# Strassen products on pairs of output stripes, with weight sums formed by adding DMAs, in a two-layer streaming-encoder kernel

## The chip, the cores and the metric

The kernel runs on one core of a Trainium2 chip, as one program. The metric is the device time of one execution in microseconds (us): 1938.96 as the median of three runs before the change (1936.39 to 1940.4). The engines that matter here are TensorE (PE; its weight loads are listed as PEld), VectorE (DVE), ScalarE (ACT), GpSimd (POOL) and SyncE (SP), which issues most DMAs. Every engine works through its own instructions in a fixed order and waits on semaphores for the others.

## The reference

A sequence of 512 positions with 16 meta tokens in front (528 rows of 2048 features) passes two layers, each with a norm ahead and a residual add behind, and a last norm.

```python
for layer in range(DEPTH):
    hn = rms_norm(h, norm_gain[layer])
    if layer % 2 == 0: y = even_mixer(...)   # ... concatenate([a_out, b_out]) @ w_out
    else:              y = odd_mixer(...)
    h = h + y
h = rms_norm(h, final_norm_gain)
return h[:, N_META:]
```

Layer 0 (even) joins a convolution branch with sparse attention and ends in a 2048 x 2048 output projection. Layer 1 (odd) is a gated linear recurrence of 16 heads with 128 features each. Its end is what the change is about:

```python
q, fz, i, g = split_last(hn @ w_in, (D_REC, D_REC, D_REC, D_REC))
...
o = o * lax.rsqrt(jnp.mean(jnp.square(o), -1, keepdims=True) + RMS_EPS)
o = o * norm_g.reshape(H_C, DV_C).astype(jnp.float32)
o = o.reshape(bsz, t_len, D_REC).astype(hn.dtype) * jax.nn.silu(g)
return o @ w_out
```

All of it is in float32, and 2048 x 2048 matrices are multiplied with that accuracy.

## The kernel before, in words

Activations lie transposed, features on the 128 partitions and positions along the row, as 16 tiles. A product with a 2048 x 2048 matrix is made of 16 *stripes*: one stripe is 128 output features, its weights are a 128 x 2048 float32 tile of 1 MB (16 blocks of 128 x 128), and its result is one PSUM bank of 512 columns or two of 264.

For accuracy each float32 operand is a pair of float16 numbers, hi and lo, and each block takes three matmuls: hi by hi, hi by lo, lo by hi (`stripe`, L233 to L235). So a stripe of layer 0 has 96 matmuls of 264 columns and a stripe of 512 positions 48 matmuls of 512 columns. What a stripe needs of its weights is done by `load`: SP fetches the tile into one of three buffers `w32` (L185); ACT squares it and sums each row (L193); POOL adds the rows' sums over the partitions (`all_sum`, L142); DVE makes a power-of-two scale and its inverse from that (L146, L199, L201); then in two halves of 1024 columns ACT writes hi, the scaled weights rounded to float16 (L207), and DVE writes lo, what is left over (L208). Tiles `wh` and `wl` have two buffers of 2048 columns. `split` (L275 on ACT, L276 on DVE) makes such pairs of activations.

The order of the work, by the profile's times: layer 0's mixer to about 740 us; its output projection, the loop at L709 over 16 stripes, to about 933. There DVE adds a finished stripe's two PSUM halves to the residual tile `h1` (L716), and ACT squares the result for layer 1's norm, into `acc1` for stripe 0 (L720) and into `sq1` for the others (L723). Its activations are the pairs `x`, split from 8 tiles `mb` and 8 tiles `z` ahead of it (L275, L276). Then the norm, the 16 recurrent heads to about 1590, 16 gate stripes to 1750.8 and layer 1's output projection. Every gate stripe is squared and scaled like any other, its sum going to a column of `gstat`; the gated heads `ON` are then split into the pairs `MO` (the name `on`) with a scale that needs all 16 sums. The output projection does stripes 0 to 13 one after another, 48 matmuls of 512 columns each; the residual comes back from `h1d` in memory by SP into a tile `fz`, DVE adds it (L977), and ACT squares the sum and applies the last gain (L983, L986). The last two stripes go in two halves of 256 columns (L1012 to L1014), with the final norm and the writing out of the first half beside the second.

Within a stage the order is set by a scheduler that works with bands of priority (`band(WGT)` for weights, `EVAC` for emptying PSUM, `SIDE`, `CONV`) and by pools with a fixed number of buffers: an instruction that writes a tile stands behind the readers of what the buffer held. The order is fixed when the program is built.

Of the kernel before, what the change touches and what calls it, by code (L numbers as in the profile page):

```python
# [11 lines left out]
F32 = mybir.dt.float32  # L12
# [62 lines left out]
def trunk_kernel(ctx: ExitStack, tc: tile.TileContext, x: bass.AP, w: bass.AP, wukv: bass.AP,  # L75
# [53 lines left out]
    warm_in = wpool.tile([128, 2048], F16, name="wl", bufs=2)[:, :512]  # L129
# [58 lines left out]
    def load(s, back, keep=None):  # L188

        w32 = load_raw(s)  # L190
        junk = wpool.tile([128, 2048], BF16, name="junk", bufs=1)
        ss = wpool.tile([128, 1], F32, name="ss", bufs=4)
        S.activation(junk, w32, AF.Square, accum_out=ss)  # L193
        total = wpool.tile([128, 1], F32, name="tot", bufs=4) if keep is None else keep
        all_sum(total, ss)
# [6 lines left out]
        sc, inv = sc.bitcast(F32), inv.bitcast(F32)  # L202
        hi = wpool.tile([128, 2048], F16, name="wh", bufs=2)
        lo = wpool.tile([128, 2048], F16, name="wl", bufs=2)
        for n in range(2):
            sl = slice(1024 * n, 1024 * (n + 1))
            S.activation(hi[:, sl], w32[:, sl], AF.Identity, scale=sc)  # L207
            V.scalar_tensor_tensor(lo[:, sl], w32[:, sl], sc, hi[:, sl], op0=OP.mult, op1=OP.subtract)  # L208
        return hi, lo, inv
# [7 lines left out]
    def stripe(s, X, back, wide=True, order=(0, 1), ring=None, keep=None):  # L217

        cols = columns(wide)
        ring = [r or bank for r in ring or (None, None)]  # L220
        parts = [(r(), sl) for r, sl in zip(ring, cols)]
        parts = [(p[:, :sl.stop - sl.start], sl) for p, sl in parts]
        with band(WGT):
            hi, lo, inv = load(s, back, keep)
        for n, half in enumerate(order):
            for o, sl in parts:
                for k in range(8):
                    kt = half * 8 + k
                    xh, xl = X[kt]
                    ws = slice(kt * 128, kt * 128 + 128)  # L230
                    if xh.shape[-1] == SEQ:
                        sl = slice(0, SEQ)
                    P.matmul(o, hi[:, ws], xh[:, sl], start=n == 0 and k == 0, stop=False)  # L233
                    P.matmul(o, hi[:, ws], xl[:, sl], start=False, stop=False)  # L234
                    P.matmul(o, lo[:, ws], xh[:, sl], start=False, stop=n == 1 and k == 7)  # L235
        return parts, inv
# [470 lines left out]
    back1 = xscale[1][1]  # L707
    H1 = []
    for n in range(KT):  # L709
# [4 lines left out]
        with band(EVAC):  # L714
            for p, sl in ps:
                V.scalar_tensor_tensor(hin[:, sl], p, inv, hin[:, sl], op0=OP.mult, op1=OP.add)  # L716
            H1.append(hin)
            Q.dma_start(h1d[n], hin)
            if n == 0:
                S.activation(acc1, hin, AF.Square)  # L720
# [71 lines left out]
    def rec_head(h, fz, q, v):  # L792
# [120 lines left out]
        on = ht([128, SEQ], F32, "on", 18)  # L913
# [43 lines left out]
    with band(SIDE):
        gs = ht([128, 2], F32, "gs")
        V.tensor_reduce(gs[:, 0:1], gstat, axis=AX, op=OP.add)
        V.scalar_tensor_tensor(gs[:, 0:1], gs[:, 0:1], 2049.0 * 128.1, vmax[:, 1:2], op0=OP.mult, op1=OP.mult)  # L960
# [3 lines left out]
        for h in range(16):  # L964
            MO.append(split(ht([128, 2, SEQ], F16, "on", 18), ON[h], gs[:, 1:2]))

    HS = SEQ // 2  # L970
# [3 lines left out]
    def add_square(n, ps, inv, sl, hin):  # L974

        h2 = H2[n]
        V.scalar_tensor_tensor(h2[:, sl], ps, inv, hin[:, sl], op0=OP.mult, op1=OP.add)  # L977
# [17 lines left out]
    for n in range(KT - 2):  # L995
        with band(EVAC):
            hin = residual(n)
        ps, inv = stripe(S_OO + n, MO, oback, wide=False)
        with band(EVAC):
            add_square(n, ps[0][0], inv, slice(0, SEQ), hin)  # L1000
    with band(WGT):
        hins = [residual(n) for n in (KT - 2, KT - 1)]
        W = {n: load(S_OO + n, oback) for n in (KT - 2, KT - 1)}
    for c in range(2):
        tk = slice(c * HS, (c + 1) * HS)
        for n in (KT - 2, KT - 1):
            p = main_ps.tile([128, 512], F32, name="mps", bufs=3)[:, :HS]
            hi, lo, inv = W[n]
            for k in range(KT):
                xh, xl = MO[k]  # L1010
                ws = slice(k * 128, k * 128 + 128)
                P.matmul(p, hi[:, ws], xh[:, tk], start=k == 0, stop=False)  # L1012
                P.matmul(p, hi[:, ws], xl[:, tk], start=False, stop=False)
                P.matmul(p, lo[:, ws], xh[:, tk], start=False, stop=k == KT - 1)  # L1014
            with band(EVAC):
                got = add_square(n, p, inv, tk, hins[n - KT + 2])
# [12 lines left out]
        with band(EVAC if c else SIDE):  # L1029
            at = 0  # L1030
            for g, size in enumerate((4, 4, 4, 2, 2) if c else (2,) * 8):
                if c == 0:
                    o = ht([128, T], F32, "fv"[g % 2], 2)
                elif g < 3:
                    o = wpool.tile([128, 2048], F32, name="w32", bufs=3)
                else:
                    o = wpool.tile([128, 2048], F16, name=("wh", "wl")[g - 3], bufs=2).bitcast(F32)
# [93 lines left out]
```

## Time and profile before

| | |
|---|---|
| median of three runs | 1938.96 us |
| the profiled execution | 1940.51 us, span 1938.7 us, granted clock 0.985 |
| PE busy | 1855.5 us, 96% |
| DVE busy | 1268.5 us, 65% |
| ACT busy | 1143.1 us, 59% |
| POOL busy | 145.2 us, 7% |
| HBM read | 177.38 MB |

Times within the profile are counted from the span's first instruction. A row of a group gives the line, the engine, the operation, what it writes and reads with buffer numbers left out, and behind the bar the busy time, the mean of one in ns, and the time that the engine had been idle just before, with what ended it. "L233 <-ACT" thus means that TensorE's matmul at line 233 had waited for ACT. A row of the time line gives the start, the duration and the instruction. Matmuls overlap, so the distance between two starts tells their price, and the duration in a row does not. Idle time of an engine other than the one that bounds a stage costs nothing.

### The profile page before, as it was taken

How to read it: one execution, taken by the hardware profiler on the slowest of the kernel's cores; microseconds unless marked ns; L12 is line 12 of the kernel's file. 1: busy time of each engine (PE TensorE's matmuls, PEld its weight loads, DVE VectorE, ACT ScalarE, POOL GpSimd, SP SyncE). 2: the span in 40 equal slices, each digit the busy share in tenths (PEclk: the TensorE clock that was granted, in tenths of full speed). 3: DMA queues.
4: the chain of work that ended last, by engine and by line, in shares of the span. 5: the costliest groups of instructions: out<-in, count | busy, mean ns of one | idle time of the engine just before them, and what ended most of it. 6: DMA issues, size and time to landing. Idle time of an engine off the chain costs nothing.

```text
span 1938.7 us, 35168 instructions
## 1 busy us (share of the span) xinstructions
PE 1855.5 (96%) x14430; PEld 1358.2 (70%) x14430; DVE 1268.5 (65%) x2729; ACT 1143.1 (59%) x1833; POOL 145.2 (7%) x294
## 2 busy tenths in 40 slices
PE   8999999799999898999899999999999999999997
PEld 6767568678888787888577777777777764444445
DVE  7588988896747355434677777677777774454335
ACT  6544565346565765434577776677767765465443
POOL 1100001011211210000100000000000000000000
PEclk9999999899999999999999999999999999999999
DMA  6322223234443235433222121221221222223333
GB/s 236 108 79 92 87 93 120 73 95 124 118 128 105 77 101 198 150 132 110 77 88 88 66 88 66 88 88 66 88 88 67 93 99 88 95 101 103 130 109 98
DMA packets 46722, 198.75 MB, mean 103 GB/s; under 512 B 5792, under 2 KB 13256, under 8 KB 27872
## 3 DMA queue, kind: packets, MB, share of 16 engines
q1 hardware_dynamic: 38000, 182.20, 26.9%
q0 software_dynamic: 8560, 14.30, 3.5%
q8 instruction: 113, 1.85, 0.4%
q14 instruction: 49, 0.40, 0.1%
HBM read 177.38 MB, written 11.22 MB: 97 GB/s over the span
## 4 chain that ended last, share of the span: by engine, by line
issue 52%; PE 18%; DMA 11%; DVE 9%; ACT 7%; POOL 3%; SPq 0%; POOLq 0%; ACTq 0%; DVEq 0%
DMA w<-in_w_dram 9%; DVE wl L208 5%; PE mps L233 4%; PE mps L234 4%; PE mps L235 4%; ACT junk L193 3%; POOL tot L142 2%; ACT wh L207 2%; DVE z L546 1%; PE po L600 1%; PE s L249 1%; DVE mask L512 1%; PE s L575 1%; DMA L<-bdram 0%; DVE mask L521 0%
## 5 line engine op out<-in xcount | busy, mean ns | idle before, releaser
L233 PE MATMUL mps<-x,wh 128*128 128x264 f16 (+1 forms) x3440 | 1021.0, 297 | 22.6 <-ACT gt L533 10.4
L234 PE MATMUL mps<-x,wh 128*128 128x264 f16 (+1 forms) x3440 | 1021.9, 297 | 5.7 <-DVE x L276 5.0
L235 PE MATMUL mps<-x,wl 128*128 128x264 f16 (+1 forms) x3440 | 1021.5, 297 | 0.0
L193 ACT ACTIVATE junk<-w 128x2048 bf16<-128x2048 f32 x144 | 275.1, 1910 | 493.5 <-DMA w<-in_w_dram 486.8
L234 PEld LDWEIGHTS <-wh 128*128 128x128 f16 x3680 | 362.2, 98 | 164.8 <-issue 26.4
L235 PEld LDWEIGHTS <-wl 128*128 128x128 f16 x3680 | 362.3, 98 | 159.8 <-issue 13.7
L233 PEld LDWEIGHTS <-wh 128*128 128x128 f16 x3680 | 362.3, 98 | 149.9 <-issue 9.6
L208 DVE SCALAR_TENSOR_TENSOR wl<-w,sc,wh 128x1024 f16<-128x1024 f32 x288 | 361.6, 1282 | 33.5 <-ACT wh L207 33.0
L207 ACT ACTIVATE wh<-w,sc 128x1024 f16<-128x1024 f32 x288 | 313.4, 1135 | 40.3 <-PE mps L234 39.7
L146 DVE TENSOR_SCALAR u<-tot 128x1 int32<-128x1 int32 x112 | 17.1, 152 | 286.1 <-POOL tot L142 286.0
L546 DVE SCALAR_TENSOR_TENSOR z<-u,vec,z 128x528 f32<-128x528 f32 x240 | 180.8, 763 | 2.7
L142 POOL PARTITION_ALL_REDUCE tot<-ss x112 | 44.7, 400 | 1185.6 <-ACT junk L193 1184.5
L235 PE MATMUL mps<-on,wl 128*128 128x512 f16 x224 | 85.0, 379 | 4.7 <-DVE wl L208 4.7
L233 PE MATMUL mps<-on,wh 128*128 128x512 f16 x224 | 84.9, 379 | 1.8 <-ACT on L275 1.4
L234 PE MATMUL mps<-on,wh 128*128 128x512 f16 x224 | 84.9, 379 | 0.0
L784 ACT ACTIVATE qhm<-q 128x256 f16<-128x256 f32 x128 | 51.8, 416 | 41.3 <-DVE q L886 41.3
L785 DVE SCALAR_TENSOR_TENSOR qlm<-q,qhm 128x256 f16<-128x256 f32 x128 | 52.3, 418 | 8.9 <-ACT qhm L784 8.6
L785 DVE SCALAR_TENSOR_TENSOR kt0l<-k,kt0h 128x512 f16<-128x512 f32 (+1 forms) x64 | 35.3, 551 | 24.5 <-ACT kt0h L784 24.4
L146 DVE TENSOR_SCALAR u<-gstat 128x1 int32<-128x1 int32 x16 | 2.4, 153 | 70.2 <-POOL gstat L142 70.2
L871 DVE COPY_PREDICATED A<-msk,s 128x256 f32<-128x256 uint8 x96 | 46.0, 479 | 0.8 <-PE s L790 0.8
L716 DVE SCALAR_TENSOR_TENSOR h<-mps,inv,h 128x264 f32<-128x264 f32 x32 | 15.5, 488 | 45.2 <-PE mps L235 45.2
L512 DVE SCALAR_TENSOR_TENSOR mask<-sq,wiT,mask 128x144 f32<-128x144 f32 (+3 forms) x80 | 36.6, 491 | 6.0 <-ACT sq L511 5.8
(365 smaller groups left out, 2394.2 us busy)
## 6 DMA issues: line engine op xcount, KB each, us to landing
w<-in_w_dram SPq DMA_DIRECT2D x146, 1024.0 KB, 4.9
h<-in_x_dram SPq DMA_DIRECT2D x16, 264.0 KB, 4.4
h1d<-h SPq DMA_DIRECT2D x16, 264.0 KB, 2.1
fz<-h1d SPq DMA_DIRECT2D x15, 256.0 KB, 2.6
z<-in_x_dram SPq DMA_DIRECT2D x8, 264.0 KB, 6.7
L<-bdram POOLq DMA_DIRECT2D x8, 264.0 KB, 3.8
L<-mask POOLq DMA_DIRECT2D x8, 264.0 KB, 3.4
mbd<-mb SPq DMA_DIRECT2D x8, 264.0 KB, 2.6
```

Source lines behind the costliest of these rows:

```text
L142: G.partition_all_reduce(out, src, channels=128, reduce_op=op or bass_isa.ReduceOp.add)
L193: S.activation(junk, w32, AF.Square, accum_out=ss)
L207: S.activation(hi[:, sl], w32[:, sl], AF.Identity, scale=sc)
L208: V.scalar_tensor_tensor(lo[:, sl], w32[:, sl], sc, hi[:, sl], op0=OP.mult, op1=OP.subtract)
L233: P.matmul(o, hi[:, ws], xh[:, sl], start=n == 0 and k == 0, stop=False)
L234: P.matmul(o, hi[:, ws], xl[:, sl], start=False, stop=False)
L235: P.matmul(o, lo[:, ws], xh[:, sl], start=False, stop=n == 1 and k == 7)
L512: V.scalar_tensor_tensor(M[t][:, s0:s1], r[:, :s1 - s0], wiT[:, t, h:h + 1], M[t][:, s0:s1], op0=OP.mult, op1=OP.add)
L546: eng.scalar_tensor_tensor(z, u[:, j:j + T], col(V_CW + i * CW + j), z, op0=OP.mult, op1=OP.add)
L784: S.activation(hi, src, AF.Copy, scale=scale)
L785: V.scalar_tensor_tensor(lo, src, scale, hi, op0=OP.mult, op1=OP.subtract)
L871: V.copy_predicated(A.rearrange("p b (n a m) -> p b n a m", a=2, m=mm)[:, :, :, 1, :], msk[:, li - 1 + i:li + i, :].rearrange("p b (n m) - ...
```

## The change

**Half buffers.** `load` is taken apart into `square_sum`, `scales` and `split_weights`; tiles `wh` and `wl` now hold 1024 columns and have five buffers each. This concerns all stripes of the kernel.

**Gate squares.** In layer 0's output projection each of the 16 stripes is followed by `gate_stat`: ACT's queue issues the load of one gate stripe's weights (1 MB, tile `gw`, two buffers), and ACT squares and sums them into a column of `gss`. One sum over the partitions for all 16 comes before the gate stage, whose stripes then take their scales from it (`known`) and are not squared again. They now go in the order 0, 8, 1, 9 and so on, and after each two of them `group` makes four pairs of operands: the two heads themselves (`MO`), and sums and differences of their halves of 256 positions (`FA`, `FB`).

**Strassen's scheme.** Stripes 0 to 13 of layer 1's output projection go in seven pairs. Two stripes, the two halves of the 2048 input features and the two halves of the 512 positions make a 2 x 2 by 2 x 2 block product, done with 7 products instead of 8; each is 8 blocks times three matmuls of 256 columns. The weight operands are the quarters w11 and w12 of the first stripe and w22 of the second, and the sums s1 = w21 + w22, s2 = s1 + w11, s4 = s2 + w12 and s3 = w11 + w21; the signs of the scheme lie with the activations' sums and with the adds behind the products. The sums are formed by DMAs that add what they bring to what lies in the tile, which GpSimd issues: s1, s2 and s4 one after the other in one tile `wt` (two buffers, for pairs n and n+1), so that L1072 must come behind the split of s1, and L1075 behind the split of s2. The residuals, all 16, are now brought by POOL's queue straight into the tiles `x` that hold the sums later (L1046), and each finished product is added to the places where it belongs, by DVE. The last two stripes and the tail are as before.

```diff
-        hi = wpool.tile([128, 2048], F16, name="wh", bufs=2)
-        lo = wpool.tile([128, 2048], F16, name="wl", bufs=2)
+        hi = wpool.tile([128, 1024], F16, name="wh", bufs=5)
+        lo = wpool.tile([128, 1024], F16, name="wl", bufs=5)
...
+    def gate_stat(h):
+        with band(CONV):
+            raw = U.tile([128, 2048], F32, name="gw", bufs=2)
+            S.dma_start(raw, w[S_G + h])
+            square_sum(raw, gss[:, h:h + 1])
...
+        gate_stat(n)
...
     def residual(n):
-        hin = ht([128, T], F32, ("fz", "fz", "k")[max(0, n - KT + 3)], 2)
-        Q.dma_start(hin[:, :SEQ], h1d[n, :, NM:])
         H2[n] = r2p.tile([128, SEQ], F32, name="x", bufs=KT)
-        return hin
+        G.dma_start(H2[n], h1d[n, :, NM:])
+
+    def pair_weights(sa, sb):
+
+        with band(WGT):
+            A_ = load_raw(sa)
+            tt = ht([128, 1024], F32, "wt", 2)
+            Q.dma_start(tt, w[sb, :, :1024])
+            G.dma_start(tt, w[sb, :, 1024:], accum_op=OP.add)
+            B_ = wpool.tile([128, 2048], F32, name="w32", bufs=3)
+            Q.dma_start(B_[:, 1024:], w[sb, :, 1024:])
+            Q.dma_start(B_[:, :1024], w[sa, :, :1024])
+            G.dma_start(B_[:, :1024], w[sb, :, :1024], accum_op=OP.add)
...
+            out["w11"] = split_weights(A_[:, :1024], sc)
+            out["s1"] = split_weights(tt, sc)
+            G.dma_start(tt, w[sa, :, :1024], accum_op=OP.add)
+            out["w12"] = split_weights(A_[:, 1024:], sc)
+            out["s2"] = split_weights(tt, sc)
+            G.dma_start(tt, w[sa, :, 1024:], accum_op=OP.add)
+            out["s3"] = split_weights(B_[:, :1024], sc)
+            out["w22"] = split_weights(B_[:, 1024:], sc)
+            out["s4"] = split_weights(tt, sc)
+        return out, inv, ninv
...
+        product(a, W["w11"], x11)
+        product(c, W["s1"], y1)
+        product(b, W["s2"], u2)
+        product(a, W["w12"], x21, start=False)
+        product(b, W["s3"], z3, start=False)
+        product(c, W["s4"], x22, start=False)
+        product(b, W["w22"], z4, start=False)
```

In the diff `w[sa]` and `w[sb]` are the two stripes of a pair; L1054, L1058, L1072 and L1075 are its four adding DMAs in the order in which they stand above, and L1053, L1056 and L1057 the plain loads by SP.

How this moves the instructions: at the start of layer 0's output projection ACT's order was this before. `h1_8496` is stripe 0's result, `w32_8748` and `w32_8873` belong to stripes 2 and 3; stripe 1's weights (`w32_8623`) were split further ahead, among the splits of `x`.

```order
L275 ACTIVATE x_8474<-z_4788,mxb_8400 128x528
L275 ACTIVATE x_8477<-z_5416,mxb_8400 128x528
L275 ACTIVATE x_8480<-z_6490,mxb_8400 128x528
L207 ACTIVATE wh_8761<-w32_8748,sc_8757 128x1024 x2
L720 ACTIVATE acc1_8495<-h1_8496 128x528
L207 ACTIVATE wh_8886<-w32_8873,sc_8882 128x1024 x2
L723 ACTIVATE sq1_8741<-h1_8619 128x528
L193 ACTIVATE junk_9125,ss_9126<-w32_9123 128x2048
```

And TensorE mixed stripe 1 (`mps_8621`) with stripe 0 (`mps_8498`, `mps_8499`), 28 matmuls of the one among the 96 of the other:

```order
L233 LDWEIGHTS wh_8513
L233 MATMUL mps_8499<-x_8459,wh_8513 128x264
L234 LDWEIGHTS wh_8636
L234 MATMUL mps_8621<-x_8456,wh_8636 128x264
L235 LDWEIGHTS wl_8637
L235 MATMUL mps_8621<-x_8456,wl_8637 128x264
```

After the change the same place of ACT's order reads as follows; `h1_8596` is stripe 0's result, `w32_8729` stripe 1's weights.

```order
L287 ACTIVATE x_8575<-z_5478,mxb_8498 128x528
L287 ACTIVATE x_8578<-z_6564,mxb_8498 128x528
L725 DMA gw_8721<-in_w_dram 128x2048
L725 DMA gw_8852<-in_w_dram 128x2048
L740 ACTIVATE acc1_8593<-h1_8596 128x528
L190 ACTIVATE junk_8723,gss_8594<-gw_8721 128x2048
L190 ACTIVATE junk_8732,ss_8731<-w32_8729 128x2048
L725 DMA gw_8983<-in_w_dram 128x2048
L190 ACTIVATE junk_8854,gss_8594<-gw_8852 128x2048
L206 ACTIVATE wh_8742<-w32_8729,sc_8738 128x1024
L206 ACTIVATE wh_8746<-w32_8729,sc_8738 128x1024
```

What moved: stripe 1's square and split now stand behind `acc1` of stripe 0 and two gate squares, and TensorE takes all of stripe 0 before the first matmul of stripe 1.

POOL's order in layer 1's output projection held one row per stripe before, the sum over the partitions:

```order
L142 ISA tot_21143<-ss_21141 128x1
L142 ISA tot_21219<-ss_21217 128x1
L142 ISA tot_21295<-ss_21293 128x1
L142 ISA tot_21371<-ss_21369 128x1
L142 ISA tot_21447<-ss_21445 128x1
```

After the change it holds the adding DMAs of two pairs at a time. `wt_21506` is the summing tile of pair 2, `wt_21757` of pair 3, `wt_22008` of pair 4; `w32_21760` and `w32_22011` hold s3 of pairs 3 and 4.

```order
L1054 DMA wt_21757<-in_w_dram 128x1024
L1072 DMA wt_21506<-in_w_dram 128x1024
L1058 DMA w32_21760<-in_w_dram 128x1024
L1075 DMA wt_21506<-in_w_dram 128x1024
L142 ISA tot_21773<-ss_21771 128x1
L1054 DMA wt_22008<-in_w_dram 128x1024
L1072 DMA wt_21757<-in_w_dram 128x1024
L1075 DMA wt_21757<-in_w_dram 128x1024
L1058 DMA w32_22011<-in_w_dram 128x1024
```

What moved: the first sum of the next pair stands ahead of the second sum of the running pair in every turn; in the first turn shown the next pair's s3 stands ahead of the running pair's s4 too (so for pairs 1, 2 and 4), in the second behind it (pairs 3 and 5). TensorE takes the products of a pair in the order w11, s1, s2, w12, s3, s4 (the last two partly mixed or exchanged), w22, the last mixed with w11 of the next pair.

More of the change, by code (lines that the diff above doesn't have):

```diff
@@ L186, in load_raw, with square_sum, scales @@
         return w32
-    def load(s, back, keep=None):
-        w32 = load_raw(s)
+    def square_sum(src, ss):
         junk = wpool.tile([128, 2048], BF16, name="junk", bufs=1)
[L192 to L195, printed above, removed]
+        S.activation(junk[:, :src.shape[-1]], src, AF.Square, accum_out=ss)
+    def scales(total, back):
         u = wpool.tile([128, 1], I32, name="u", bufs=4)
@@ L201, in load, with split_weights @@
         V.tensor_scalar(inv, u, back, None, op0=OP.add)
-        sc, inv = sc.bitcast(F32), inv.bitcast(F32)
-        hi = wpool.tile([128, 2048], F16, name="wh", bufs=2)
-        lo = wpool.tile([128, 2048], F16, name="wl", bufs=2)
[L205 to L209, printed above, removed]
+        return sc.bitcast(F32), inv.bitcast(F32)
+    def split_weights(src, sc):
+        hi = wpool.tile([128, 1024], F16, name="wh", bufs=5)
+        lo = wpool.tile([128, 1024], F16, name="wl", bufs=5)
+        S.activation(hi, src, AF.Identity, scale=sc)
+        V.scalar_tensor_tensor(lo, src, sc, hi, op0=OP.mult, op1=OP.subtract)
+        return hi, lo
+    def load(s, back, keep=None, known=None):
+        w32 = load_raw(s)
+        if known is None:
+            ss = wpool.tile([128, 1], F32, name="ss", bufs=4)
+            square_sum(w32, ss)
+            total = wpool.tile([128, 1], F32, name="tot", bufs=4) if keep is None else keep
+            all_sum(total, ss)
+            known = scales(total, back)
+        sc, inv = known
+        halves = [split_weights(w32[:, 1024 * n:1024 * (n + 1)], sc) for n in range(2)]
+        return [h[0] for h in halves], [h[1] for h in halves], inv
     def bank():
@@ L215, in columns, with stripe @@
         return (slice(0, HT), slice(HT, T)) if wide else (slice(NM, T),)
-    def stripe(s, X, back, wide=True, order=(0, 1), ring=None, keep=None):
+    def stripe(s, X, back, wide=True, order=(0, 1), ring=None, keep=None, known=None):
         cols = columns(wide)
@@ L223, in stripe @@
         with band(WGT):
-            hi, lo, inv = load(s, back, keep)
+            hi, lo, inv = load(s, back, keep, known)
         for n, half in enumerate(order):
@@ new lines, in pair_weights @@
+    def pair_weights(sa, sb):
[8 more added lines that the diff above has]
+            G.dma_start(B_[:, :1024], w[sb, :, :1024], accum_op=OP.add)
+            ss = wpool.tile([128, 3], F32, name="ss3", bufs=2)
+            for i, v in enumerate((A_, tt, B_[:, 1024:])):
+                square_sum(v, ss[:, i:i + 1])
+            s1 = wpool.tile([128, 1], F32, name="ss", bufs=4)
+            V.tensor_reduce(s1, ss, axis=AX, op=OP.add)
+            total = wpool.tile([128, 1], F32, name="tot", bufs=4)
+            all_sum(total, s1)
+            sc, inv = scales(total, oback)
+            ninv = wpool.tile([128, 1], F32, name="ninv", bufs=4)
+            V.tensor_scalar(ninv, inv, -1.0, None, op0=OP.mult)
+            out = {}
+            out["w11"] = split_weights(A_[:, :1024], sc)
[8 more added lines that the diff above has]
+        return out, inv, ninv
@@ new lines, in product, with cut @@
+    def product(p, ws, xs, start=True, stop=True, resume=True):
+        hi, lo = ws
+        for k in range(8):
+            sl = slice(k * 128, k * 128 + 128)
+            xh, xl = xs[k]
+            for i, (wt, xt) in enumerate(((hi, xh), (hi, xl), (lo, xh))):
+                P.matmul(p, wt[:, sl], xt, start=start and k == i == 0, stop=stop and k == 7 and i == 2,
+                         skip_group_check=stop and not start and resume)
+    def cut(X, sl):
+        return [(xh[:, sl], xl[:, sl]) for xh, xl in X]
@@ L1001, in trunk_kernel @@
+    for n in range(0, KT - 2, 2):
+        pair_stripes(n)
     with band(WGT):
-        hins = [residual(n) for n in (KT - 2, KT - 1)]
+        for n in (KT - 2, KT - 1):
+            residual(n)
         W = {n: load(S_OO + n, oback) for n in (KT - 2, KT - 1)}
@@ L1006, in trunk_kernel @@
         for n in (KT - 2, KT - 1):
-            p = main_ps.tile([128, 512], F32, name="mps", bufs=3)[:, :HS]
+            p = bank()[:, :HS]
             hi, lo, inv = W[n]
[L1009 to L1014, printed above, removed]
+            for half in range(2):
+                product(p, (hi[half], lo[half]), cut(MO[8 * half:8 * half + 8], tk), half == 0, half == 1, False)
             with band(EVAC):
-                got = add_square(n, p, inv, tk, hins[n - KT + 2])
+                V.scalar_tensor_tensor(H2[n][:, tk], p, inv, H2[n][:, tk], op0=OP.mult, op1=OP.add)
+                got = add_square(n, tk)
         with band(EVAC):
@@ L1032, in trunk_kernel @@
                 if c == 0:
[L1033 removed]
+                    o = ht([128, T], F32, "ta" if g % 2 else "fz", 2)
                 elif g < 3:
```

120 lines of the change are left out of this document (89 added, 31 removed).

## The prediction

> **What bounds the kernel now.** I read the busy times by stage first, then the groups of the last projection by form, then the rows around the places that the change touches.
>
> ```profile
> PE 1855.5 (96%) x14430; PEld 1358.2 (70%) x14430; DVE 1268.5 (65%) x2729; ACT 1143.1 (59%) x1833; POOL 145.2 (7%) x294
> 740.00:760.00 20.00, 15.13 (x111) 11.46 (x109) 9.69 (x15) 12.16 (x17) 0.77 (x2) 0.87 0.62 222
> 760.00:880.00 120.00, 120.00 (x1060) 104.03 (x1059) 54.97 (x101) 53.58 (x61) 3.85 (x10) 0.99 0.41 143
> 1590.00:1750.80 160.80, 159.75 (x795) 75.01 (x793) 82.35 (x148) 94.80 (x115) 5.39 (x14) 1.00 0.27 93
> 1750.80:1903.70 152.90, 146.45 (x673) 65.18 (x672) 59.22 (x97) 74.07 (x85) 5.01 (x13) 1.00 0.32 112
> ```
>
> The columns of a stage are its length, then PE, PEld, DVE, ACT and POOL busy, the granted clock, the DMA share and GB/s. TensorE bounds nearly everything: 120 of 120 in layer 0's output projection, 159.75 of 160.80 in the gates, 146.45 of 152.90 in layer 1's projection, while ACT and DVE are about half busy. So less work on another engine buys nothing; fewer matmul columns, or a new wait of TensorE, is what moves the end.
>
> ```profile
> L235 PE MATMUL mps<-on,wl 128*128 128x512 f16 x224 | 85.0, 379 | 4.7 <-DVE wl L208 4.7
> L233 PE MATMUL mps<-on,wh 128*128 128x512 f16 x224 | 84.9, 379 | 1.8 <-ACT on L275 1.4 <-ACT wh L207 0.4
> L208 DVE SCALAR_TENSOR_TENSOR wl<-w,sc,wh 128x1024 f16<-128x1024 f32 x28 | 34.6, 1278 | 0.3 <-ACT wh L207 0.2
> L207 ACT ACTIVATE wh<-w,sc 128x1024 f16<-128x1024 f32 x29 | 31.6, 1133 | 6.1 <-PE mps L234 6.1
> L193 ACT ACTIVATE junk<-w 128x2048 bf16<-128x2048 f32 x13 | 24.8, 1911 | 69.9 <-DMA w<-in_w_dram 69.9
> L193 ACT ACTIVATION_READ_ACCUMULATOR junk<-w 128x1 f32 x13 | 2.4, 186 | 0.0
> 1750.84 0.38 PE L233 MATMUL mps<-on,wh 128*128 128x512 f16 x1
> 1751.05 0.38 PE L234 MATMUL mps<-on,wh 128*128 128x512 f16 x1
> 1753.64 0.38 PE L234 MATMUL mps<-on,wh 128*128 128x512 f16 x1
> 1905.34 0.27 PE L1012 MATMUL mps<-on,wh 128*128 128x256 f16 x1
> 1907.96 0.27 PE L1012 MATMUL mps<-on,wh 128*128 128x256 f16 x1
> ```
>
> The last projection's 14 full stripes run from 1750.84 to the first 256-column matmul at 1903.70 (the window's end), 152.9 us. Between 1751.05 and 1753.64 lie 12 matmuls of 512 columns, 0.216 us each; between 1905.34 and 1907.96 lie 24 of 256 columns, 0.109 us each. Halving the columns halves the price, so Strassen's 7 for 8 arrives whole in matmul time. 14 x 48 x 0.216 = 145.1; the other 7.8 us are waits, most for the splits (4.7 and 1.8 in the rows).
>
> **Layer 1's projection.** Seven pairs of 7 x 24 = 168 matmuls, 18.3 us a pair and 2.62 us a product: 128.2 us. If nothing else bound it, that is 24.7 us less than 152.9. Whether it does hangs on the four sums of a pair that GpSimd's accumulating DMAs (512 KB each) put together, two of which (L1072, L1075) sit inside the pair: s2 may be added to the tile only when s1 is split, s4 only when s2 is split. An accumulate of that size from memory is not in the trace of before. The nearest rows are those of the bias tiles (L569), one of which ran alone:
>
> ```profile
> 622.56 0.85 POOL L569 DMA_DIRECT2D L<-mask  x1 [3.29 <-DMA L<-bdram]
> L<-mask POOLq DMA_DIRECT2D x1, 200.0 KB, 2.9
> GB/s 0 0 0 0 0 0 0 118 389 389 372 439 355 102 0 38 205 166 192 192 192 192 205 205 52 0 0 0 0 0 0 0 0 0 0 0 0 131 0 0
> w<-in_wukv_dram SPq DMA_DIRECT2D x4, 512.0 KB, 3.6
> w<-in_w_dram SPq DMA_DIRECT2D x146, 1024.0 KB, 4.9
> ```
>
> The GB/s row is the window 622 to 627 in 40 slices: first a plain copy at about 389, then the accumulate at 192 to 205, half as fast. 200 KB at 195 take 1.05 of its 2.9 us, so 1.85 are latency; 512 KB take 2.7 at that rate and 1.35 at the plain one. I take 2.7, from the one accumulate that I found running alone.
>
> Now one turn, in time from the end of the lo split of s4 of pair n-1. The summing tile has two buffers, so the load of pair n+1's tile starts only here: 3.6 us (the 512 KB row). On POOL's queue L1054 of pair n+1 stands ahead of L1072 of pair n and waits for that load, so both leave from 3.6 on, 0.85 apart: data of the first from 5.45 to 8.15, of L1072 to 10.85. The split of s2 (1.13 + 1.28) is ready at 13.3. TensorE has s4, w22 of pair n-1 and w11, s1 of pair n to do meanwhile, 4 x 2.62 = 10.5: **it waits 2.8 us**. From 13.3 it does s2, w12, s3, to 21.15. L1075 leaves at 13.3, lands at 17.85, and s4 is split at 20.3: no further wait. That is the order for pairs 3, 5 and 6. For pairs 1, 2 and 4 L1058 of the next pair stands ahead of L1075: L1075 then lands at 20.55 and s4 is ready at 23.0, 1.85 more. Six turns: 3 x 2.8 + 3 x 4.65 = 22.4 us of waits. Pair 0 has its tile early and waits for its splits as before (the 1.4 of the row). Collisions with the 2.5 MB that SP loads in a turn are not excluded (2.62 MB at 389 and 2.1 MB at 195 make 17.5 us of transfers in a turn of 21 to 23); I put 0.5 us a turn, 3 in all. 128.2 + 22.4 + 1.4 + 3 = 155.0, **2 us more than before**. Ends: at the plain rate, s2 is ready at 10.55 and s4 never late, 129.9 us (-23); the upper end is the third rival's.
>
> ACT does some 15 us of work a pair (4.4 squares, 7 x 1.13, evacuation), DVE 15 (7 x 1.28, adds): both under a turn of 21, so neither is the bound unless the waits vanish. The last two stripes and the tail stay.
>
> By the Trainium skill, "DMA: Bandwidth & Descriptors", section "Anatomy of one DMA", a GpSimd DMA takes 2.0 us plus its bytes at 436 GB/s, accumulate or not: 3.2 us for 512 KB, and 2.5 for the 200 KB that took 2.9. By that rule the projection would take about 130 us and the first rival holds; the row at 192 to 205 GB/s speaks against it.
>
> **Gate squares in layer 0's projection.** In the gate stage their removal is worth nothing, since TensorE is busy 159.75 of 160.80; the added splits and 256-column adds there fit into the time that ACT and DVE have free. In layer 0's projection 16 squares of 2.1 us go onto ACT, 53.58 of 120 busy, and a second megabyte per stripe onto the DMA (143 GB/s): covered, but for the beginning.
>
> ```profile
> 756.34 1.91 ACT L193 ACTIVATE junk<-w 128x2048 bf16<-128x2048 f32 x1 [3.84 <-DMA w<-in_w_dram]
> 759.50 5.10 ACT L275 ACTIVATE x<-z,mxb 128x528 f16<-128x528 f32 x8
> 770.49 0.63 ACT L720 ACTIVATE acc<-h 128x528 f32<-128x528 f32 x1
> 759.01 0.82 PE L233 MATMUL mps<-x,wh 128*128 128x264 f16 x3 [2.65 <-ACT x L275]
> 761.31 0.42 PE L235 MATMUL mps<-x,wl 128*128 128x264 f16 x1
> 762.57 0.28 PE L235 MATMUL mps<-x,wl 128*128 128x264 f16 x1
> 768.51 0.49 DVE L716 SCALAR_TENSOR_TENSOR h<-mps,inv,h 128x264 f32<-128x264 f32 x1 [0.18 <-PE mps L235]
> 784.26 0.49 DVE L716 SCALAR_TENSOR_TENSOR h<-mps,inv,h 128x264 f32<-128x264 f32 x1 [1.48 <-PE mps L235]
> 786.96 0.49 DVE L716 SCALAR_TENSOR_TENSOR h<-mps,inv,h 128x264 f32<-128x264 f32 x1 [2.21 <-PE mps L235]
> 797.76 0.49 DVE L716 SCALAR_TENSOR_TENSOR h<-mps,inv,h 128x264 f32<-128x264 f32 x1 [2.21 <-PE mps L235]
> 925.98 0.49 DVE L716 SCALAR_TENSOR_TENSOR h<-mps,inv,h 128x264 f32<-128x264 f32 x1 [2.25 <-PE mps L235]
> ```
>
> Before, stripe 0 ends at 768.5 with 28 matmuls of stripe 1 among its own (by the order of the instructions), because stripe 1's weights were squared and split ahead of it; later stripes follow every 10.8 us (786.96, 797.76), and the last ends 2.7 after 925.98, at 928.7. After, ACT has acc1, which needs stripe 0 evacuated, and the first gate square ahead of stripe 1's own square. So stripe 0 ends, without those 28 matmuls (3.1 us) and without the wait of 2.65 behind the square of 756.34, at about 763; then come evacuation 0.5, acc1 0.63, three squares of 2.1, hi 1.13 and lo 1.28: 9.9 us in which TensorE has nothing, since stripe 1 is next in its order. After the wait of 2.65 the matmuls took 0.42 instead of 0.28 until about 761.9, a loss of some 1.1. 763 + 9.9 + 1.1 + 15 x 10.8 = 936, and the 1.2 or so that one later stripe waits in either kernel: **7 to 8.5, I take 8 us**. Ends: +2 if layer 0's splits come 6 us sooner, +11 if the gate weights, sent for by ACT only behind its last split, land 3 us late (4.9 for a load).
>
> By the Trainium skill, "TensorE: Matmul & The Clock Gate", section "What's actually happening", the clock halves after an idle window of about 3.4 us and stays so for about 3.4 us of work: that would be 1.7 in place of my 1.1, and the sum 0.6 higher. The slow matmuls at 761.31 agree in kind.
>
> **Half buffers in layer 0.** They change the order on all engines; TensorE's largest wait there is this:
>
> ```profile
> L233 PE MATMUL mps<-x,wh 128*128 128x264 f16 (+1 forms) x3440 | 1021.0, 297 | 22.6 <-ACT gt L533 10.4
> ```
>
> I cannot price an order: below, half of these 10.4 us may go; above, the same may come. 0, with 5 either way.
>
> **Sum.** 2 + 8 + 0 = +10. The profiled execution took 1940.5 (span 1938.7), 1.5 above the median of 1938.96; +10 gives 1950.5 there and 1949 for the median, which I forecast. Its own range is 1941 to 1957.
>
> **Rivals.** What a measurement can tell from no change is 0.2%, 3.9 us.
> - *Accumulates at the plain rate* (faster). Then TensorE never waits for a sum: -23 + 8 = -15, 1924; at 250 GB/s, with 2.1 us an accumulate, the same steps leave 11 us of waits (-9 and +8, no gain). It decides at about 2 us for 512 KB. For it: the skill's rule, and that no accumulate from memory was seen. Against: the 192 to 205. Chance 0.29 with all rates fast enough for a gain.
> - *No bubble in layer 0* (same). The reordering brings stripe 0 five to eight us sooner, and the projection is as forecast: 1941. The wait at 756.34 for a load speaks for it. 0.15.
> - *Sums behind loads* (slower still). An accumulate issued 0.2 us after a megabyte load landed late:
>
> ```profile
> 589.18 0.87 POOL L569 DMA_DIRECT2D L<-mask  x1 [2.94 <-DMA L<-bdram]
> L<-mask POOLq DMA_DIRECT2D x1, 264.0 KB, 7.2
> ```
>
> Alone it would take 1.85 + 1.4, so this is 4 us more. If half of the six turns meet that, 12 in place of my 3: 1958; all six, 1970. 0.15.
> - The forecast: 0.41.
>
> **How the numbers follow.** Faster: 0.29 and a little of the second rival, 0.30. Same: the rest of that rival and the low end of the forecast, 0.17. Slower: 0.53. The range leaves out about half of the fast case below 1924 and the worst of the third rival above 1961.
>
> **What would show it.** In the projection: waits of TensorE's s2 products for DVE's lo split (L207 of the new lines) of about 3 us a pair, and of s4 in pairs 1, 2, 4 of about 2; L1072 landing 6 to 7 us after its issue. In layer 0: one wait of about 10 us between the first two stripes, behind ACT's squares. If the pairs follow every 18.3 us, or that wait isn't there, the step is wrong.

## The result, and the profile after

The changed kernel takes 1965.5 us (median of 4 runs, 1962.6 to 1968.8) against 1938.4 before: ratio 1.014, 95% interval 1.0121 to 1.016. It is slower by 27 us, where 10 had been forecast; the direction was right, and the time lies above the range. The profiled execution, the quickest of the four, has a span of 1960.8, 22.1 more than before; the sums by stage below are for it.

By stage, length first, then PE, PEld, DVE, ACT and POOL busy, clock, DMA share, GB/s; the stages are layer 0's output projection from the end of its first stripe, the recurrent heads with the gates, the seven pairs, and the last two stripes with the tail:

```profile
747.50:931.50 184.00, 166.73 (x1443) 142.80 (x1442) 75.94 (x135) 112.36 (x117) 7.36 (x19) 0.94 0.62 225
946.80:1735.30 788.50, 781.30 (x6608) 549.44 (x6607) 589.58 (x1285) 535.33 (x874) 33.17 (x78) 1.00 0.26 91
1735.30:1925.80 190.50, 146.16 (x1180) 121.42 (x1179) 99.71 (x160) 99.93 (x123) 29.47 (x38) 0.88 0.64 162
1925.80:1960.80 35.00, 22.98 (x201) 19.76 (x198) 14.94 (x41) 8.05 (x15) 0.00 (x0) 0.87 0.36 121
```

Layer 0's projection ends at 931.5 instead of 928.6, so everything up to there costs 3 us. From there to the last projection pass 803.8 us where 822.2 passed before (928.6 to 1750.84): 18 won, in a part where the buffers are halved, the gates' order is changed, the gate squares are gone and the forms' sums and splits have come in. The pairs take 190.5 us where the 14 stripes took 152.9: 37.6 lost. The tail is the same 35. 3 - 18.4 + 37.6 = 22.2. So the small sum hides large terms of both signs, unlike the forecast's. In the pairs' row TensorE is busy 146.2 us, where the 7 x 18.3 us of matmuls at full rate make 128.2: 44 us of the 190.5 are waits and some 18 are matmuls at a lower granted clock (0.88); for these 18 the forecast had put nothing.

The first loss, in layer 0, on ACT's time line:

```profile
PE mps L245 <- ACT wh L206: 14.1, 1, 14.1
748.40 0.64 ACT L740 ACTIVATE acc<-h 128x528 f32<-128x528 f32 x1 [4.14 <-DVE h L736]
753.49 1.91 ACT L190 ACTIVATE junk<-gw 128x2048 bf16<-128x2048 f32 x1 [4.45 <-DMA gw<-in_w_dram]
755.59 1.91 ACT L190 ACTIVATE junk<-w 128x2048 bf16<-128x2048 f32 x1
757.62 1.91 ACT L190 ACTIVATE junk<-gw 128x2048 bf16<-128x2048 f32 x1
759.53 2.17 ACT L206 ACTIVATE wh<-w,sc 128x1024 f16<-128x1024 f32 x2
761.76 0.40 PE L245 MATMUL mps<-x,wh 128*128 128x264 f16 x1 [14.09 <-ACT wh L206]
761.95 0.43 PE L246 MATMUL mps<-x,wh 128*128 128x264 f16 x1
762.17 0.43 PE L245 MATMUL mps<-x,wh 128*128 128x264 f16 x1
```

TensorE stands for 14.1 us: acc1, then 4.45 for the first gate weights, which ACT sent for only behind its last split (at 745.52), then three squares and the split, one after the other. Then the matmuls run at half speed: they start 0.22 us apart, and 0.11 apart only from 767.3 on.

The larger loss is in the pairs. Below is ACT's evacuation of w11, which comes once a pair, so the distances are the turns; and one turn's DMA issues on POOL and SP with what ACT waits for.

```profile
1740.26 0.45 ACT L1112 ACTIVATE ta<-mps,inv 128x256 f32<-128x256 f32 x1
1776.14 0.45 ACT L1112 ACTIVATE ta<-mps,inv 128x256 f32<-128x256 f32 x1
1803.11 0.45 ACT L1112 ACTIVATE ta<-mps,inv 128x256 f32<-128x256 f32 x1
1830.23 0.46 ACT L1112 ACTIVATE ta<-mps,inv 128x256 f32<-128x256 f32 x1
1912.96 0.45 ACT L1112 ACTIVATE ta<-mps,inv 128x256 f32<-128x256 f32 x1
1782.31 0.33 SPq L1053 DMA_DIRECT2D wt<-in_w_dram  x1
1786.49 0.87 POOL L1054 DMA_DIRECT2D wt<-in_w_dram  x1 [10.15 <-DMA wt<-in_w_dram]
1787.05 1.20 POOL L1072 DMA_DIRECT2D wt<-in_w_dram  x1
1787.32 0.33 SPq L1056 DMA_DIRECT2D w<-in_w_dram  x1
1787.70 0.42 SPq L1057 DMA_DIRECT2D w<-in_w_dram  x1
1798.42 1.15 ACT L206 ACTIVATE wh<-wt,sc 128x1024 f16<-128x1024 f32 x1 [3.55 <-DMA wt<-in_w_dram]
1799.62 0.61 PE L1087 MATMUL mps<-kt0l,wh 128*128 128x256 f16 x2 [5.63 <-ACT wh L206]
1801.18 0.86 POOL L1075 DMA_DIRECT2D wt<-in_w_dram  x1 [1.68 <-DVE wl L207]
1806.77 1.15 ACT L206 ACTIVATE wh<-wt,sc 128x1024 f16<-128x1024 f32 x1 [2.60 <-DMA wt<-in_w_dram]
1809.27 0.33 SPq L1053 DMA_DIRECT2D wt<-in_w_dram  x1
```

From the load at 1782.31 to the next at 1809.27 the forecast's loop can be followed step by step: load 4.2 (to POOL's issue), L1054 and L1072 until 1798.42, 11.9; split 2.8; L1075 5.6; split 2.5: 27.0 us. The five turns from 1776.14 to 1912.96 take 27.4 in the mean (27.0, 27.1, 25.3, 31.0, 26.4), where 21 to 23 and half a microsecond were forecast; only the first of them is followed here. The turn ahead of them, 1740.26 to 1776.14, takes 35.9. There L1075 of pair 0 is issued among the 16 residual transfers of 256 KB that POOL's queue sends from 1726.26 to 1744.6, and lands after 10.6 us:

```profile
1740.79 1.22 POOL L1075 DMA_DIRECT2D wt<-in_w_dram  x1
1751.43 1.15 ACT L206 ACTIVATE wh<-wt,sc 128x1024 f16<-128x1024 f32 x1 [5.02 <-DMA wt<-in_w_dram]
1752.64 0.61 PE L1087 MATMUL mps<-on,wh 128*128 128x256 f16 x2 [5.01 <-ACT wh L206]
```

That the residuals make this add late is read from these rows; no run moved them away. The forecast had no term for them.

### The profile page after: what moved, and what is told of

It is laid out like the page before. It is cut to its first block, busy times and chain, and to the rows that moved or that the text cites. A ratio compares the mean times of both kernels' runs of the same rounds, so it can differ in the third digit from the quotient of the medians.

```text
span 1960.8 us, 36523 instructions
## 1 busy us (share of the span) xinstructions
PE 1843.4 (94%) x14934; PEld 1412.9 (72%) x14934; DVE 1346.1 (69%) x2788; ACT 1194.5 (61%) x1893; POOL 176.4 (9%) x316
## 5 line engine op out<-in xcount | busy, mean ns | idle before, releaser
L245 PE MATMUL mps<-x,wh 128*128 128x264 f16 (+1 forms) x3440 | 1020.3, 297 | 26.8 <-ACT wh L206 14.1
L245 PEld LDWEIGHTS <-wh 128*128 128x128 f16 x3456 | 339.8, 98 | 139.4 <-ACT wh L206 14.4
L246 PEld LDWEIGHTS <-wh 128*128 128x128 f16 x3456 | 339.9, 98 | 128.3 <-issue 15.9
L247 PEld LDWEIGHTS <-wl 128*128 128x128 f16 x3456 | 339.7, 98 | 121.7 <-issue 9.7
L207 DVE SCALAR_TENSOR_TENSOR wl<-w,sc,wh 128x1024 f16<-128x1024 f32 x256 | 329.0, 1287 | 130.8 <-ACT wh L206 125.9
L190 ACT ACTIVATE junk<-w 128x2048 bf16<-128x2048 f32 (+2 forms) x132 | 240.6, 1823 | 153.9 <-DMA w<-in_w_dram 145.7
L1087 PEld LDWEIGHTS <-wh 128*128 128x128 f16 x912 | 93.4, 103 | 59.8 <-ACT wh L206 31.7
L1087 PE MATMUL mps<-on,wh 128*128 128x256 f16 x464 | 78.9, 274 | 14.3 <-ACT wh L206 11.6
L207 DVE SCALAR_TENSOR_TENSOR wl<-w,gsc,wh 128x1024 f16<-128x1024 f32 x32 | 41.1, 1283 | 37.2 <-ACT wh L206 36.4
L207 DVE SCALAR_TENSOR_TENSOR wl<-wt,sc,wh 128x1024 f16<-128x1024 f32 x21 | 26.9, 1283 | 54.5 <-ACT wh L206 54.3
L1087 PE MATMUL mps<-on,wl 128*128 128x256 f16 x232 | 63.2, 273 | 0.0
L806 DVE SCALAR_TENSOR_TENSOR qlm<-q,qhm 128x256 f16<-128x256 f32 x128 | 52.4, 420 | 14.1 <-ACT qhm L805 12.1
L206 ACT ACTIVATE wh<-w,gsc 128x1024 f16<-128x1024 f32 x32 | 36.6, 1145 | 39.6 <-PE mps L246 39.4
L1087 PEld LDWEIGHTS <-wl 128*128 128x128 f16 x456 | 46.9, 103 | 11.8 <-DVE wl L207 3.6
L206 ACT ACTIVATE wh<-wt,sc 128x1024 f16<-128x1024 f32 x21 | 24.0, 1142 | 43.6 <-DMA wt<-in_w_dram 43.6
```

Source lines behind the costliest of these rows:

```text
L190: S.activation(junk[:, :src.shape[-1]], src, AF.Square, accum_out=ss)
L206: S.activation(hi, src, AF.Identity, scale=sc)
L207: V.scalar_tensor_tensor(lo, src, sc, hi, op0=OP.mult, op1=OP.subtract)
L245: P.matmul(o, hi[half][:, ws], xh[:, sl], start=n == 0 and k == 0, stop=False)
L246: P.matmul(o, hi[half][:, ws], xl[:, sl], start=False, stop=False)
L247: P.matmul(o, lo[half][:, ws], xh[:, sl], start=False, stop=n == 1 and k == 7)
```

## The experiments

The theory after the result: (a) half buffers made the gains, in layer 0 and in the recurrent part; (b) the gate squares' place makes the wait of 14 us; (c) the loop over the summing tile makes the turn of 27 us. The main rivals: the gains come from the gate squares' move; the pairs are held by ACT's and DVE's work. The kernel before was measured again beside each experiment, at 1941.2 to 1942.6 us instead of the 1938.4 beside the changed kernel; differences to the changed kernel below are taken from the medians and good to some 4 us. Ratios are to the kernel before.

**e1, half buffers alone**, on the kernel before:

```diff
...
-        hi = wpool.tile([128, 2048], F16, name="wh", bufs=2)
...
+            hi = wpool.tile([128, 1024], F16, name="wh", bufs=5)
...
```

> The kernel before with nothing changed but the weights' pairs in halves of 1024 columns, five buffers each. Theory (the half buffers made the whole gain ahead of the last projection, 18 us in layer 0's mixer and 18 in the recurrent stage): 1938 - 36 = 1902, say 1898 to 1910, layer 0's first output stripe done at about 748. Rival (the gain comes from what the gate squares' move does to the order): 1930 to 1942.

Measured: 1905.3 us (1903.4 to 1907.2), ratio 0.981, interval 0.9787 to 0.9833. One place differs from the expectation: layer 0's first stripe was done at 758.6, not 748, since stripe 1 is again mixed in, but the last one at 916.3 instead of 928.6, 12 us sooner, and the last projection begins at 1719.1, another 19 won. So (a) holds, and half buffers alone beat both kernels. The last projection, 149.2 us, is 3.7 shorter too.

**e9, the same with four buffers** in place of five, as many bytes as before:

> The kernel before with halves of 1024 columns and four buffers each, so as many bytes as before. If the finer grain makes the gain (a half comes free when its own matmuls are done): 1903 to 1912, like the five buffers' 1905. If the added fifth buffer makes it: 1922 to 1940.

Measured: 1906.3 us (two runs; 0.9823, 0.9761 to 0.9885). The finer grain makes the gain, not the room. What TensorE waited for between 1000 and 1600, before, and then the same stretch before, in e9 and in e1:

```profile
PE s L904 <- ACT kk L896: 2.7, 2, 1.8
PE s L922 <- ACT sh L917: 2.7, 7, 1.2
PE s L788 <- ACT qhm L784: 1.5, 2, 1.1
PE s L907 <- DVE e L888: 1.5, 5, 0.4
```
```profile
1000.00:1600.00 600.00, 590.77 (x5515) 447.56 (x5511) 434.47 (x1062) 423.88 (x716) 19.28 (x59) 1.00 0.23 81
```
```profile
1000.00:1600.00 600.00, 599.08 (x5546) 452.10 (x5545) 450.15 (x1059) 436.55 (x726) 19.89 (x59) 1.00 0.24 83
```
```profile
1000.00:1600.00 600.00, 600.00 (x5549) 451.32 (x5547) 456.67 (x1062) 433.59 (x720) 20.68 (x60) 1.00 0.24 84
```

Before, these are waits of the heads' own small matmuls for ACT and DVE; with halves TensorE has none in e1. Before, ACT wrote a stripe's two halves one behind the other (a time line prints them as one row, x2); in e1 one half comes every 6 us or so (1001.12, 1007.54, 1013.55), with the heads' instructions between. That this is the way the gain comes is read from these rows and was not tried by itself. The waits are only half of the gain there: from the end of layer 0's projection to the start of the last one e1 has 9.9 us less of them, and its matmuls, as many as before, are busy 9.5 us less; why they are is not shown.

**e2, gate squares later**, on the changed kernel:

```diff
-        gate_stat(n)
+        if 4 <= n < 12:
+            gate_stat(2 * n - 8)
+            gate_stat(2 * n - 7)
```

> The changed kernel with the 16 gate squares issued two at a time behind stripes 4 to 11 of layer 0's projection, not one behind each. Theory (the wait of 14 us between stripes 0 and 1 is ACT's queue of squares): that wait falls below 4 us and the time by 12 to 18, to 1948 to 1953. Rival (stripe 1's weights come late for another reason, a load or the half buffers): the wait stays over 8 us, 1960 to 1966.

Measured: 1951.6 us (1951.3 to 1955.7), 14 less than the changed kernel. TensorE has no wait between 755 and 775, layer 0's projection ends at 917.9, within 2 us of e1's 916.3, and the last projection begins at 1721.6 (e1: 1719.1). So (b) holds: it was the place, and the squares' work itself costs nothing that can be seen.

**e3, Strassen taken back**, on the changed kernel: the 14 stripes as before, residuals still on POOL's queue; the forms that `group` makes are left out too.

```diff
...
-    for n in range(0, KT - 2, 2):
-        pair_stripes(n)
+    for n in range(KT - 2):
+        with band(EVAC):
+            residual(n)
+        ps, inv = stripe(S_OO + n, MO, oback, wide=False)
+        with band(EVAC):
+            V.scalar_tensor_tensor(H2[n], ps[0][0], inv, H2[n], op0=OP.mult, op1=OP.add)
+            add_square(n, slice(0, SEQ))
```

> The changed kernel with Strassen's pairs taken back: 14 full stripes of 512 columns in layer 1's projection, no forms and no sums; half buffers, gate squares and the residuals on POOL's queue stay. Theory (the pairs cost 37 us against the stripes): 1928, say 1922 to 1932, the projection's 14 stripes in 148 to 154 us. Rival (half of the loss is the residuals' burst or the half buffers there): 1940 to 1950.

Measured: 1926.6 us (1925.0 to 1929.8; 0.9923, 0.9901 to 0.9944), 39 less than the changed kernel. Its stripes run from 1748.32 to the first 256-column matmul at 1893.36, 145.0 us, without one wait. That is a point that the forecast missed: half buffers can take away the 7.8 us of waits of the plain stripes too (e9's stripes also take 145.0 us, e1's 149.2), so that Strassen's products could save 145.0 - 128.2 = 17 us at most, and as built cost 45. (The parts ahead of the projection took 13 us longer than in the changed kernel. Some 11 of these are there at the end of layer 0's projection, 943 instead of 931.5, and 8 at the end of its first stripe, where the code is the same: its order came out otherwise. Such differences of order lie on all comparisons here.)

**e7, plain loads** in place of adding ones, so that the products are of other weights:

```diff
-            G.dma_start(tt, w[sa, :, :1024], accum_op=OP.add)
+            G.dma_start(tt, w[sa, :, :1024])
```

and the other three likewise.

> The changed kernel with the four DMAs of a pair bringing the same 512 KB without adding (so the sums are not formed and the products are of other weights; every wait and queue stays). Theory (a turn of 27 us is the chain load, two adds, split, add, split, with adds at 140 GB/s): the turn falls to 19 to 21 us and the time by 36 to 48, to 1918 to 1930. Rival (the turn is set by ACT's and DVE's work or by POOL's issuing): the turn stays above 25, 1955 to 1966.

Measured in a single run: 1929.0 us, 36 less. The turn fell to 21.9 in the mean (1770.03 to 1879.58 in five), not to 19 to 21, but far from 25: the adding costs 5.5 us a turn, with every wait and queue kept. The first turn is still 31.1.

**e6, three summing tiles**, on the changed kernel:

```diff
...
-            tt = ht([128, 1024], F32, "wt", 2)
+            tt = ht([128, 1024], F32, "wt", 3)
```

> The changed kernel with three summing tiles in place of two (two small scale tiles share room to make place). Theory (the load of the next tile waits for the split of s4 two pairs back, and with L1054 ahead of L1072 closes the loop of 27 us): the loop opens, and a turn is what the DMAs need, four adds at some 3.6 us and 2.6 MB at 389 GB/s, 21 to 23 us: 1930 to 1942. Rival (the adds' own time inside a pair, L1072 and L1075 behind the splits, is enough for 27): over 1955.

Measured: 1961.2 us (two runs). The rival's number, but not its reason. The scheduler used the third tile to bring the load one pair further ahead, so L1054 is now of the pair after the next and still stands directly ahead of L1072 (1796.45 and 1797.01 below, behind a wait of 11.28). By these rows the loop was only lengthened by a pair. In the last two turns, where no further L1054 and no loads for it stand there, the turn was 20.9 and 21.3.

```profile
1791.24 0.33 SPq L1053 DMA_DIRECT2D wt<-in_w_dram  x1
1796.45 0.89 POOL L1054 DMA_DIRECT2D wt<-in_w_dram  x1 [11.28 <-DMA wt<-in_w_dram]
1797.01 1.20 POOL L1072 DMA_DIRECT2D wt<-in_w_dram  x1
1878.51 0.86 POOL L1072 DMA_DIRECT2D wt<-in_w_dram  x1 [9.43 <-DVE wl L207]
1869.84 0.45 ACT L1112 ACTIVATE ta<-mps,inv 128x256 f32<-128x256 f32 x1
1890.70 0.45 ACT L1112 ACTIVATE ta<-mps,inv 128x256 f32<-128x256 f32 x1
```

**e13, s1 by DVE**, so that no L1054 is left on POOL's queue; s2, s3, s4 by adding DMAs:

```diff
-            G.dma_start(tt, w[sb, :, 1024:], accum_op=OP.add)
...
+            V.tensor_tensor(tt, tt, B_[:, 1024:], op=OP.add)
```

> The changed kernel with s1 alone formed by DVE (one add a pair) and s2, s3, s4 by adding DMAs as before. So L1072 has no L1054 of the next pair ahead of it on POOL's queue, but the two adds inside a pair stay. Theory (the loop of 27 us closes through that place on the queue): the turn falls to 19.5 to 22, the time to 1918 to 1936. Rival (the two adds inside the pair, 5.5 us each, and the load on the DMA engines hold it by themselves): 1950 to 1965.

Measured: 1939.1 us (1932.6 to 1943.9), between the two; the turn fell to 23.1 (from 27.4), the first one to 28.7 (from 35.9). The time from issue to landing of L1072, minimum, median and maximum, in the changed kernel, in e13 and in e7:

```profile
DMA to landing us min/median/max: 5.6/9.3/11.3
```
```profile
DMA to landing us min/median/max: 5.4/5.6/6.2
```
```profile
DMA to landing us min/median/max: 3.8/4.8/8.8
```

Without L1054 and the loads that come with it, the same 512 KB add lands in 5.6; which of the two had made it late, this run does not part. So (c) holds for 4.3 of the 27 us. What holds the turn at 23 it does not show: in the next run the two adds inside a pair are gone too, and the turn is 22.5.

**e10, s2 and s4 by DVE**, s1 and s3 by adding DMAs:

```diff
-            G.dma_start(tt, w[sa, :, :1024], accum_op=OP.add)
+            V.tensor_tensor(tt, tt, A_[:, :1024], op=OP.add)
```

and the same for s4. **e8v**: all four by DVE, from plainly loaded stripes. **e8**: all four by GpSimd's adds.

> The other half: s2 and s4 formed by DVE (two adds a pair), s1 and s3, which are needed early and by nothing inside the pair, by adding DMAs. Theory: the chain of a pair holds no DMA, two adds in a turn pass beside the loads, and DVE has 15 + 2.6 us a pair: a turn of 18.5 to 20.5, the time 1912 to 1926. Rival (any adding DMA beside the loads is too slow): 1940 or more.

> The same sums made by DVE's adds. Four more adds of about 1.3 us on an engine with 15 us a pair: a turn of 19.5 to 21.5, bound by DVE, 1917 to 1930. Rival (DVE's queue puts the adds ahead of what TensorE waits for): 1940 or more.

> The changed kernel with the four sums made by GpSimd's adds of tiles already loaded, no adding DMA and 2 MB of loads a pair in place of 2.5 MB and four adds. Theory (only the adding DMAs hold the pairs up): a turn of 18.3 to 20 us, 1910 to 1925. Rival (GpSimd's adds of 1024 columns, with its change between two kinds of work, are as slow as the DMAs, 3 us or more each in the chain): 1935 to 1960.

Measured: e10 1930.8 us (1930.2 to 1938.0), e8v 1934.7 (1929.1 to 1940.5), e8 1988.3 (two runs). e10 and e8v both lie between their expectation and its rival, with turns of 22.5 and 23.1: the loop is gone, and something else holds the pairs at 22. e10's first turn is 21.2, as short as the others. Of e10's 22.5 us, 18.3 are the matmuls at full rate, some 2.6 are waits and some 1.6 are matmuls at a lower granted clock (0.94). In e10 TensorE now waits for DVE's adds out of PSUM, with three banks shared by neighbouring pairs:

```profile
PE mps L1087 <- DVE x L1107: 12.8, 7, 6.2
PE mps L1087 <- ACT ta L1112: 1.8, 2, 1.2
```

In e8 the rival holds, and beyond its range: an add took 2.34, but where GpSimd goes from the sum over the partitions to an add and back, it stands for 5.9 to 7.6 us in which the profile shows no wait:

```profile
1820.45 2.35 POOL L1055 TENSOR_TENSOR w<-w,w 128x1024 f32<-128x1024 f32 x1
1828.76 0.40 POOL L142 PARTITION_ALL_REDUCE tot<-ss  x1 [5.96 <-issue]
1836.15 2.34 POOL L1069 TENSOR_TENSOR wt<-wt,w 128x1024 f32<-128x1024 f32 x1 [6.99 <-issue]
```

**e11, e10 with the later gate squares of e2**, and **e14, that with four more PSUM banks**, from the heads' pool, for every second pair:

```diff
-        a, b, c = [bank()[:, :HS] for _ in range(3)]
+        a, b, c = [(ps1 if n % 4 else bank)()[:, :HS] for _ in range(3)]
```

> The run before with the gate squares two at a time behind stripes 4 to 11. Theory (the two costs add): 14 us less than that run, 1898 to 1912, and below the 1905 of the half buffers alone if the pairs pass at 19 us or less. Rival (they don't add): 1912 to 1926.

> The run with inner sums on DVE and later gate squares (1914 to 1923), where every second pair takes its three PSUM banks from the four that the recurrent heads have left free. Theory (what is left of the pairs' waits, some 10 us behind DVE's adds out of PSUM, comes from three banks shared by neighbouring pairs): the waits for those adds go and the turn falls from 22 to 19 or 20: 1900 to 1910. Rival (the adds are late because DVE's queue waits for splits and sums, so a free bank changes nothing): 1912 to 1924.

Measured: e11 1921.5 us (1914.3 to 1923.0; 0.9905, 0.9884 to 0.9927), about 9 less than e10, the time of its rival; the two intervals do not exclude the 14 expected. e14 took 1915.4 (1911.1 to 1916.3; 0.9858, 0.9839 to 0.9878). In e14 the waits for the adds out of PSUM fell from 10.5 to 5.6, but the turn stayed at 22.0 (1776.46 to 1864.53 in four) and the time is the rival's. TensorE is busy 76.15 of these 88 us:

```profile
1776.50:1864.50 88.00, 76.15 (x653) 64.31 (x651) 65.26 (x101) 56.77 (x72) 8.45 (x12) 0.96 0.60 157
```

What holds the pairs at 22 us, once no sum does, stays open: the waits left are several and small, some 3 us a turn together, no engine is busy all the time, and no run took one of them alone. None of the versions with pairs came below the 1905 of e1.

## Why the prediction was wrong

- **The loop over the summing tile** was the right mechanism, at the right place, with a size too small; this is the term that failed, 2 us forecast and 37.6 measured: 155.0 against 190.5 us for the pairs, and for the six turns 135 against 172.7. TensorE's waits for s2 in the first three turns were 4.6, 5.6 and 5.0 us, not 2.8. Two steps of the loop were short. First, an add that is alone on the queue lands after 5.4 to 5.6 us, not 4.55; the row of the bias tile, from which I took the latency, was not quite of an add alone, since a plain copy of 264 KB moved in the same window just ahead of it. Once under way it moves mostly at about 200 GB/s, as the bias tile's did, but it starts unevenly and needs 3.7 us for its 512 KB, not 2.7; this is L1075 of the last pair, issued at 1909.37, in the window 1909 to 1916 in 40 slices:

```profile
GB/s 0 0 0 0 0 0 0 0 0 94 0 187 0 70 187 234 47 211 211 164 211 187 234 164 257 187 94 187 23 140 0 0 0 0 0 0 0 0 0 47
wt<-in_w_dram POOLq DMA_DIRECT2D x1, 512.0 KB, 5.4
```

- Second, and larger: I let L1072 land 7.25 us after L1054's issue; it took 11.9. I had SP's loads of w22 and s3 (L1056, L1057) done by then. They wait for w12's split, which DVE does behind the splits of s4 and s1, and were issued at 1787.3, just beside the two adds: four transfers of 512 KB at a time. In the window 1782 to 1806 they move together at 160 to 280 GB/s:

```profile
GB/s 0 0 212 335 246 109 0 0 0 0 102 164 205 232 225 232 178 259 219 246 225 259 280 232 253 178 7 0 0 0 55 68 191 198 198 212 184 218 212 205
```

  That is the third rival, sums behind loads: from its issue to the split L1072 takes 10.3, 11.4, 11.0 and 9.4 us in four of the six turns, and 6.6 and 5.7 in the other two. It had 0.15, and its price of 4 us a turn was about right: 4.65 too much here, and 4.3 less in e13. That its 1958 to 1970 holds the measured time is luck all the same, since it too put the half buffers at 0.
- The rest of the pairs' loss is not this loop as I priced it. The first turn took 35.9 us, 12 more than forecast, with an add of 10.6 us among the residuals. And 18.3 us a pair, which the sum starts from, was reached in the mean by no run: with the loop loosened or gone the turn is 21.9 (e7), 23.1 (e13) and 22.5 us (e10), and why stays open.
- **The first rival** (adds as fast as plain transfers) fell: e7, in which they are plain, wins 36 us. Its price fell as well: plain transfers did not bring the pairs to 130 us, their turn was 21.9. By the Trainium skill, "DMA: Bandwidth & Descriptors", section "Anatomy of one DMA", a GpSimd DMA of 512 KB would take 3.2 us (an estimate from its sum, which does not speak of adding). The add took 5.4 to 5.6, and the same transfer without adding 3.8 at least, 4.8 in the median. So the section's sum doesn't hold for an add; the measurement decides.
- **The gate squares** were priced at +8, as 9.9 us of wait and 1.1 of slow clock. Against e1, whose projection in layer 0 ends at 916.3, the changed kernel's ends at 931.5: 15.2; e2 wins 13.6 of that back. The wait is 14.1; the 9.9 are there (acc1, three squares, the split), and the rest is the 4.45 for the late gate weights, which I had named as an upper end of 3 and left out of the value. Stripe 0 ended at 747.5, not at 763; so it did come sooner, as the second rival said, but the wait came all the same. The slow matmuls came as well, from 761.76 to 767.16 behind 14.1 us without work: about 2.5 us lost, not 1.1 (half of these 5.4 us, less a wait of 0.41). By the Trainium skill, "TensorE: Matmul & The Clock Gate", section "What's actually happening", the clock is back at full speed after about 3.4 us of sustained work; the profile agrees in kind, with 5.4 us here.
- **The half buffers** were put at 0 with 5 either way; alone they are worth 33 to 36 us (e1). I looked only at the one wait of 10.4 in layer 0 and took the recurrent part, 611.8 us busy of 620, to be full. Its 8 us of waits in the rows of L904, L922, L788 and L907 were there to be seen, and the order showed ACT's halves going from one block to two. They make 8 of the 33 to 36 us; what makes the rest is shown only in part.
- **The gate stage and the tail** came as said: no wait of TensorE in the gates, 35 us behind the pairs.
- The sign came out right by cancelling, which is luck: some 31 us won ahead of the last projection (12 and 19 in e1) by a part that I had put at 0 stand against some 53 lost (37.6 and 15.2) by the two that I had put at 10.

## What to carry to other kernels

Where a tile is filled by one engine and emptied by another while TensorE is the bound, try halving the tile before anything larger: at equal bytes it was worth 35 us here, and it also took away a third of what the larger change was to save (7.8 of 24.7 us). A scheme that saves matmuls by forming sums should have the sums off the path that closes a loop: write that loop down with all that shares its queues and its engines, loads included, and look at where in each queue the next turn's work stands ahead of this turn's. Here even that did not bring a turn down to the 18.3 us of its matmuls. Price a long sum by its terms against runs that hold one term each; two errors of 30 to 40 us each looked like one of 17 here.

## What the runs showed of the hardware that I had not expected

- An adding DMA of 512 KB from memory, alone: 5.4 to 5.6 us; the same bytes without adding, 3.8 at least (e7), and SP's plain load of the same size (L1053) 3.5 at least, 3.6 in the median.
- GpSimd stands 5.9 to 7.6 us between a sum over the partitions and an elementwise add, in each direction (e8), with no releaser in the profile.
- A GpSimd add of 128 x 1024 float32 took 2.34 us.
